# Low parts of three of five up-projection operands: from VectorE to GpSimd, behind the first two differences

## The chip, the cores and the metric

The kernel runs on one core of a Trainium2 chip. The core has five engines with a queue each: TensorE (PE, with its weight loads as PEld), VectorE (DVE), ScalarE (ACT), GpSimd (POOL) and SyncE (SP, which here only starts transfers). Each engine works its queue in order and waits where an operand is not ready. The metric is the device time of one execution in microseconds; several runs are taken and the median is compared.

## The reference

One layer of a hybrid encoder over 1024 positions of width 1024, in float32. After the mixing of tokens comes the part that matters here:

```
h = layer_norm(x) * (1.0 + sc2) + sh2
u = causal_depthwise_conv(h @ w_up, conv_w, conv_b)      # w_up: 1024 x 5632
a, val = split(u, 2)
y = (silu(a) * val) @ w_down                             # 2816 x 1024
x = layer_norm(alpha * x + (1.0 + g2) * y, ln2_g, ln2_b)
```

`h @ w_up` is the up-projection. `h` is its left operand: 1024 positions, in two halves of 512.

## The kernel before

**Two parts of a number.** TensorE multiplies a rounded 32-bit format. To keep the accuracy of float32 the kernel splits each operand in a high part (the operand rounded, made by a cast) and a low part (operand minus high part, a subtraction), and makes three products: high by high, high by low, low by high (`mm3`, `product` at L851, matmuls at L859). A low part is a 128x512 subtraction with both operands in SBUF, the core's on-chip memory.

**Seven products in place of eight.** The up-projection is done by a scheme of Strassen's kind over 2x2 blocks: position halves by halves of the 1024 inputs. From the first half of the positions come `h_11` and `h_21`; from the second half come `h_22` and, by differences with the first, `h_t1 = x - h11`, `h_t2 = y - t1`, `h_t3 = y - x` and `h_t4 = h21 - t2`, where x and y are the two blocks of the second half. Each operand is four 128x512 tiles (`k` or `j` = 0 to 3) with a high and a low part.

**How they are made.** `turned_1` (L1028) is a generator of four steps. Step j loads two tiles of the first half back from memory (SP queue), transposes two blocks on TensorE into PSUM (its accumulator memory), moves them to SBUF with ScalarE (`turned`, L1006: tiles `h`), and calls `put` five times. `put` (L1010) takes a triple of engines: the first makes the difference (L1013, tile `ht`), the second the cast to the high part (L1015, tile `hc`), the third the low part (L1016, tile `hc`). Tiles `h` have four buffers, `ht` six, `hf` (the reloaded ones) four.

**What runs beside them.** The eight `head` calls (L884) do the products of `h_11` and `h_21` with one block of weights each, which need nothing of the second half: two chains of twelve matmuls per head. The weights of a head are loaded by SP, cast by ScalarE (L847) and get their low parts from VectorE (L848, called from `ready`, L868, with `lo=ve`; tiles `wh`, `wl`). A head's results go from PSUM to SBUF by ScalarE (L894) and by a VectorE addition that reads PSUM (L897, tile `mc`). The first step of `turned_1` is issued ahead of the head with number 2, and the three others behind the heads 2, 3 and 4:

```
turns = turned_1(x1)
next(turns)
for c in range(EARLY, HEAD):      # 2 to 7
    head(c)
    next(turns, None)
```

**What follows.** Then come 22 blocks (`Block`, L1159), the rest of the up-projection and the convolution. The first block uses `h_t2`, `h_t1`, `h_t3`, `h_22`, `h_t4` in this order. The weights of the blocks get their low parts from GpSimd (L848 with `lo=po`, tiles `wx`, `wh`, `wl`). Most `wx` tiles lie in memory that the pools of the steps have given back.

**What sets the order.** The program is traced in the order of the code, and a planner then orders the instructions of each engine's queue once, before the run: by the order of the code where an instruction can start by its model of the costs, and with later instructions moved ahead where it can't. Semaphores between the engines are set by the data and by the reuse of buffers. On the chip each queue stays as it was planned.

Of the kernel before, what the change touches and what calls it, by code (L numbers as in the profile page):

```python
# [15 lines left out]
ALU = mybir.AluOpType  # L16
# [28 lines left out]
def body(ctx, tc, a, out):  # L45
    nc = tc.nc
    ve, se, pe, po, sy = nc.vector, nc.scalar, nc.tensor, nc.gpsimd, nc.sync
    uid = [0]

    def nm(s):  # L50
        uid[0] += 1
        return f"{s}_{uid[0]}"

    def opened(**kw):
        cm = tc.tile_pool(reuse_waits="tile", **kw)
        return cm, cm.__enter__()
# [139 lines left out]
    def halves(half):  # L196
        return slice(half * H, (half + 1) * H)
# [615 lines left out]
    def operands(pool, name):  # L813
        return [[pool.tile([P, H], F32R, name=f"{name}{c}{k}", tag=f"{name}{c}{k}") for c in range(2)] for k in range(4)]
# [87 lines left out]
    if True:  # L902
# [98 lines left out]
        def turned(tiles, j, psp=mxt, tag="tt"):  # L1001
            ps = psp.tile([P, H], F32, name=nm("pst"), tag=tag)
            for t in range(4):
                pe.transpose(ps[:, t * P : (t + 1) * P], tiles[t][:, j * P : (j + 1) * P], ident)
            h32 = mxb.tile([P, H], F32, name=nm("h32"), tag="h32", bufs=4)
            se.activation(out=h32, in_=ps, func=AF.Identity, scale=modc[:, 4 * KD + j : 4 * KD + j + 1],  # L1006
                          bias=modc[:, 3 * KD + j : 3 * KD + j + 1])
            return h32

        def put(dst, x, y=None, op=None, e=(ve, ve, po), pool=mxb, n=2):  # L1010
            if y is not None:
                t = pool.tile([P, H], F32, name=nm("ht"), tag="ht", bufs=n)
                e[0].tensor_tensor(out=t, in0=x, in1=y, op=op)  # L1013
                x = t
            (e[1].copy if e[1] is se else e[1].tensor_copy)(out=dst[0], in_=x)  # L1015
            e[2].tensor_sub(out=dst[1], in0=x, in1=dst[0])  # L1016
            return x
# [10 lines left out]
        def turned_1(tiles):  # L1028
            for j in range(4):
                h11, h21 = [th.tile([P, H], F32, name=nm("hf"), tag="hf", bufs=4) for _ in range(2)]  # L1030
                sy.dma_start(out=h11, in_=hx[j])
                sy.dma_start(out=h21, in_=hx[j + 4])
                x, y = turned(tiles, j), turned(tiles, j + 4)
                put(h_22[j], y, e=(None, se, ve))
                t1 = put(h_t1[j], x, h11, ALU.subtract, (ve, se, ve), th, 6)
                t2 = put(h_t2[j], y, t1, ALU.subtract, (ve, se, ve), th, 6)
                put(h_t3[j], y, x, ALU.subtract, (ve, se, ve), th, 6)
                put(h_t4[j], h21, t2, ALU.subtract, (ve, se, ve), th, 6)
                yield

        m0 = merge(0, o0, iter(()))
# [43 lines left out]
    h_22, h_t1, h_t2, h_t3, h_t4 = [operands(hbp, f"hc{i}") for i in range(5)]  # L1085
    th_cm, th = opened(name="th", bufs=2)
    turns = turned_1(x1)
    next(turns)
    start = summed(order[0], slice(0, 4, 3), hbp, "fs"), raw(order[1], 1, hbp, "fs")
# [206 lines left out]
    with tc.tile_pool(name="dn", bufs=2, reuse_waits="tile") as dn:  # L1296
# [44 lines left out]
        for p in products:  # L1341
# [27 lines left out]
            for t in range(4):  # L1369
                for w in ws:  # L1370
                    down(ps, t, w, False, w is ws[-1], not fresh)
                if p == "P4":
                    z = dn.tile([P, H], F32, name=nm("z"), tag="z", bufs=2)
                    y, n0 = ys[4 + t], halves(0)
# [12 lines left out]
            elif p in ("P3", "P2", "P7"):  # L1387
                for t in range(4):
                    x = {"P3": u2, "P2": p1, "P7": p5}[p][t]
# [70 lines left out]
```

## Time and profile before

| what | us |
|---|---|
| runs: median (lowest to highest of 3) | 1549.76 (1547.07 to 1550.41) |
| profiled execution: span from first to last instruction | 1548.2 |
| profiled execution: time beside its span | none given; the span lies within the runs |
| TensorE busy (share of the span) | 1502.7 (97%) |
| VectorE | 1034.5 (67%) |
| ScalarE | 709.5 (46%) |
| GpSimd | 658.2 (43%) |

The profile is of one execution. Instructions are named by engine, line and tiles (`out<-in`), with buffer numbers left out; the many matmuls of L859 are therefore told apart by their weights' tile (`wh`, `wl`, `wx`) and by `ha`, `hb` (the first half's operands) and `hc` (the five of the second half). A time in front of a row is its start from the beginning of the span. In brackets behind a row stands how long the engine sat idle before it, and what it waited for. The mean granted clock of TensorE is 1.00 at full speed.

### The profile page before, as it was taken

How to read it: one execution, taken by the hardware profiler on the slowest of the kernel's cores; microseconds unless marked ns; L12 is line 12 of the kernel's file. 1: busy time of each engine (PE TensorE's matmuls, PEld its weight loads, DVE VectorE, ACT ScalarE, POOL GpSimd, SP SyncE). 2: the span in 40 equal slices, each digit the busy share in tenths (PEclk: the TensorE clock that was granted, in tenths of full speed). 3: DMA queues.
4: the chain of work that ended last, by engine and by line, in shares of the span. 5: the costliest groups of instructions: out<-in, count | busy, mean ns of one | idle time of the engine just before them, and what ended most of it. 6: DMA issues, size and time to landing. Idle time of an engine off the chain costs nothing.

```text
span 1548.2 us, 21760 instructions
## 1 busy us (share of the span) xinstructions
PE 1502.7 (97%) x7663; PEld 1264.7 (82%) x7663; DVE 1034.5 (67%) x2038; ACT 709.5 (46%) x1316; POOL 658.2 (43%) x607
## 2 busy tenths in 40 slices
PE   6999999999999999999998999999999999999996
PEld 3788898889889888888886877888888888888885
DVE  6756566566656565554468587777778776845798
ACT  3545555554544454442112165544544554555451
POOL 0039897787878776730000005454455443000000
PEclk9999999999999999999999999999999999999998
DMA  9156666756576578758999575443344322697552
GB/s 366 50 165 215 217 192 198 218 194 216 189 233 220 189 260 299 260 151 292 308 323 347 214 258 190 140 154 132 122 140 147 115 102 104 246 328 255 191 190 75
DMA packets 129756, 317.54 MB, mean 205 GB/s; under 512 B 13024, under 2 KB 21936, under 8 KB 129648
## 3 DMA queue, kind: packets, MB, share of 16 engines
q1 hardware_dynamic: 90208, 197.83, 37.8%
q0 software_dynamic: 25344, 92.02, 17.8%
q10 hardware_dynamic: 14096, 26.31, 4.8%
q8 instruction: 60, 0.98, 0.3%
q14 instruction: 48, 0.39, 0.1%
HBM read 223.47 MB, written 84.25 MB: 199 GB/s over the span
## 4 chain that ended last, share of the span: by engine, by line
PE 72%; POOL 9%; DMA 8%; DVE 7%; issue 2%; ACT 1%; SPq 0%; ACTq 0%; DVEq 0%; POOLq 0%
PE psu L859 25%; PE psd L1277 4%; PE psd L1278 4%; PE psd L1276 4%; PE pso L508 3%; DMA wod<-dr 3%; PE psg L192 3%; PE psg L194 3%; PE psg L193 3%; POOL dr L553 2%; PE pst L494 2%; POOL acc L559 2%; POOL dr L556 2%; PE psq L194 2%; DMA brd<-dr 2%
## 5 line engine op out<-in xcount | busy, mean ns | idle before, releaser
L859 PE MATMUL psu<-hc,wx 128*128 128x512 f32 x792 | 185.7, 389 | 0.1
L859 PEld LDWEIGHTS psu<-hc,wx 128*128 128x128 f32 x792 | 148.6, 188 | 31.3 <-ACT u L1202 0.5
L1125 DVE SCALAR_TENSOR_TENSOR pcv<-u,convp,pcv 128x1024 f32<-128x1024 f32 x88 | 113.1, 1286 | 45.4 <-ACT pcv L1123 44.4
L1266 DVE TENSOR_TENSOR op<-rw,op 128x512 fp32r<-128x512 f32 x146 | 93.4, 687 | 52.8 <-ACT op L1265 52.5
L1265 ACT CAST op<-rw 128x512 fp32r<-128x512 f32 x146 | 85.2, 622 | 85.4 <-PE psd L1278 39.8
L457 ACT ACTIVATE s<-s,mx 128x640 f32<-128x640 f32 (+7 forms) x128 | 94.5, 738 | 58.6 <-DVE mx L451 57.4
L1277 PE MATMUL psd<-op,op 128*128 128x512 f32 x292 | 113.6, 389 | 0.9 <-DVE op L1266 0.9
L1278 PE MATMUL psd<-op,op 128*128 128x512 f32 x292 | 113.6, 389 | 0.0
L1276 PE MATMUL psd<-op,op 128*128 128x512 f32 x292 | 113.1, 389 | 0.0
L497 ACT CAST pt<-pst 128x512 fp32r<-128x512 f32 (+1 forms) x192 | 82.1, 450 | 62.3 <-PE pst L494 60.8
L498 DVE TENSOR_TENSOR pt<-pst,pt 128x512 fp32r<-128x512 f32 (+1 forms) x192 | 96.0, 519 | 17.2 <-ACT pt L497 15.5
L192 PE MATMUL psq<-h1h,wh 128*128 128x512 f32 x256 | 103.8, 407 | 1.7 <-DVE h1h L188 1.3
L192 PE MATMUL psg<-h1h,wh 128*128 128x512 f32 x256 | 103.7, 405 | 0.0
L194 PE MATMUL psq<-h1h,wl 128*128 128x512 f32 x256 | 100.9, 394 | 0.9 <-DVE wl L112 0.9
L194 PE MATMUL psg<-h1h,wl 128*128 128x512 f32 x256 | 100.3, 392 | 0.5 <-DVE wl L112 0.5
L193 PE MATMUL psq<-h1l,wh 128*128 128x512 f32 x256 | 100.8, 394 | 0.0
L193 PE MATMUL psg<-h1l,wh 128*128 128x512 f32 x256 | 100.2, 391 | 0.0
L556 POOL TENSOR_SCALAR dr<-dr,cond 128x512 f32<-128x512 f32 x56 | 89.9, 1607 | 8.1 <-DMA dr<-in_w_ada 7.1
L508 PE MATMUL pso<-pt,vs 128*128 128x256 f32 x608 | 90.4, 288 | 1.3 <-DVE pt L498 1.2
L994 POOL DMA_DIRECT2D xd<-xr x8 | 4.4, 545 | 199.3 <-DVE xr L992 199.3
L508 PEld LDWEIGHTS pso<-pt,vs 128*128 128x128 f32 x608 | 81.1, 191 | 8.7 <-DVE pt L498 2.6
L112 DVE TENSOR_TENSOR wl<-ws,wh 128x1024 fp32r<-128x1024 f32 x38 | 61.2, 1611 | 39.1 <-ACT wh L111 39.1
(286 smaller groups left out, 4001.3 us busy)
## 6 DMA issues: line engine op xcount, KB each, us to landing
ws<-in_w_up SPq DMA_DIRECT2D x34, 512.0 KB, 3.7
dr<-in_w_ada POOLq DMA_DIRECT2D x32, 512.0 KB, 4.8
dr<-in_w_down POOLq DMA_DIRECT2D x22, 512.0 KB, 4.8
td<-dr POOLq DMA_DIRECT2D x22, 512.0 KB, 4.7
rw<-td SPq DMA_DIRECT2D x44, 256.0 KB, 4.5
yd<-y SPq DMA_DIRECT2D x20, 512.0 KB, 2.7
rw<-yd SPq DMA_DIRECT2D x40, 256.0 KB, 4.2
rw<-sd SPq DMA_DIRECT2D x33, 256.0 KB, 4.6
```

The costliest lines, as they stand in the source:

```text
L192: pe.matmul(ps, wh, xh, start=start, stop=False)
L193: pe.matmul(ps, wh, xl, start=False, stop=False)
L194: pe.matmul(ps, wl, xh, start=False, stop=stop)
L457: se.activation(out=st[:, 0:nk], in_=st[:, 0:nk], func=AF.Exp, scale=-1.0, bias=prev, accum_out=sums[:, col : col + 1])
L498: ve.tensor_sub(out=dl, in0=src, in1=dh)
L508: pe.matmul(ps[:, 0:256], vs[:, h % 2, j0 + j, :], pt[j // 4][:, c, j % 4, :], start=j == 0 and c == 0, stop=j == nj - 1 and c == 1)
L556: po.tensor_scalar_mul(x[:, k % 2, :] if k else acc, x[:, k % 2, :], cond[:, k : k + 1])
L859: pe.matmul(ps, w[:, a_, k, :], h[k][b_], start=first, stop=k == 3 and a_ == 1, skip_group_check=on)
L1125: ve.scalar_tensor_tensor(out=ps, in0=u[b][:, 2 - d : S + 2 - d], scalar=cp[:, 2 - d : 3 - d], in1=ps, op0=ALU.mult, op1=ALU.add)
L1276: pe.matmul(ps[t], g[:, 0, ts], d[:, 0], start=start, stop=False, skip_group_check=on)
L1277: pe.matmul(ps[t], g[:, 0, ts], d[:, 1], start=False, stop=False, skip_group_check=on)
L1278: pe.matmul(ps[t], g[:, 1, ts], d[:, 0], start=False, stop=stop, skip_group_check=on)
```

## The change

In each of the four steps the `put` of `h_22` moves from in front of `h_t1` and `h_t2` to behind them, and the low parts of `h_22`, `h_t3` and `h_t4` are subtracted by GpSimd (`po`) where VectorE (`ve`) did it. The differences stay on VectorE, the casts on ScalarE. In all twelve 128x512 subtractions change their engine, four casts and their subtractions change their place. No transfer, no buffer and no arithmetic changes.

```
                 x, y = turned(tiles, j), turned(tiles, j + 4)
-                put(h_22[j], y, e=(None, se, ve))
                 t1 = put(h_t1[j], x, h11, ALU.subtract, (ve, se, ve), th, 6)
                 t2 = put(h_t2[j], y, t1, ALU.subtract, (ve, se, ve), th, 6)
-                put(h_t3[j], y, x, ALU.subtract, (ve, se, ve), th, 6)
-                put(h_t4[j], h21, t2, ALU.subtract, (ve, se, ve), th, 6)
+                put(h_22[j], y, e=(None, se, po))
+                put(h_t3[j], y, x, ALU.subtract, (ve, se, po), th, 6)
+                put(h_t4[j], h21, t2, ALU.subtract, (ve, se, po), th, 6)
                 yield
```

## The prediction

> **What bounds the kernel now.** I read the page first (span and busy shares), then the busy time by stretches of time, to find the stage that the change touches, then the chain of work that ended last in that stage, and last the order of single instructions there.
>
> ```profile
> span 1548.2 us, 21760 instructions
> PE 1502.7 (97%) x7663; PEld 1264.7 (82%) x7663; DVE 1034.5 (67%) x2038; ACT 709.5 (46%) x1316; POOL 658.2 (43%) x607
> ```
>
> TensorE is busy for 97% of the span, so a change that only moves VectorE work pays only where TensorE waits for VectorE. The low parts of the five operands are made between 918 and 946 us (columns: length, then busy time and count of PE, PEld, DVE, ACT, POOL, then the granted clock, DMA share, GB/s):
>
> ```profile
> 905.00:918.00 13.00, 13.00 (x62) 10.41 (x61) 9.90 (x41) 8.41 (x14) 0.53 (x1) 1.00 0.91 308
> 918.00:946.00 28.00, 24.55 (x110) 19.16 (x109) 27.18 (x45) 23.37 (x43) 0.98 (x1) 0.94 0.56 192
> 946.00:978.00 32.00, 31.95 (x142) 26.09 (x141) 17.38 (x19) 15.09 (x23) 22.87 (x21) 1.00 0.49 167
> 1020.00:1320.00 300.00, 300.00 (x1325) 248.50 (x1324) 224.99 (x236) 148.70 (x212) 142.15 (x105) 1.00 0.37 128
> ```
>
> In this stretch, and not before or behind it, VectorE is the full engine: 27.18 of 28 us. TensorE has 3.45 us of idle time (28 - 24.55) and GpSimd does nothing until its end. Behind it TensorE runs without a gap (31.95 of 32, 300 of 300), so whatever is won or lost at 946 us reaches the end. The chain agrees: it leaves TensorE here, goes from difference (L1013) to low part (L1016) to the heads' weights (L848) on VectorE, and returns to TensorE at 945.02:
>
> ```profile
> 922.61 0.69 DVE hc L1016
> ...
> 944.37 0.61 DVE wh L848
> 944.98 0.04 issue
> 945.02 31.55 PE psu L859 x138
> ```
>
> TensorE's own row order shows what it waits for:
>
> ```profile
> 928.90 0.66 PE L1004 MATMUL pst<-ident,x 128*128 128x128 f32 x4 [1.10 <-ACT h L1006]
> 931.18 4.15 PE L859 MATMUL psu<-ha,wh 128*128 128x512 f32 x10 [1.63 <-DVE wh L848]
> 935.17 2.47 PE L859 MATMUL psu<-hb,wl 128*128 128x512 f32 x10
> 938.77 2.81 PE L859 MATMUL psu<-ha,wh 128*128 128x512 f32 x11 [0.22 <-ACT wh L847]
> 945.02 2.60 PE L859 MATMUL psu<-ha,wh 128*128 128x512 f32 x10 [0.50 <-DVE wh L848]
> ```
>
> It waits for low parts of the **heads'** weights, which stand in VectorE's queue behind the operands' differences. The ten products at 931.18 took 4.15 us where ten take 2.47 at 935.17: 1.7 us lost to a lower granted clock (0.55, next row).
>
> ```profile
> 931.20:935.00 3.80, 3.80 (x10) 2.97 (x11) 3.80 (x7) 3.02 (x6) 0.00 (x0) 0.55 0.74 259
> ```
>
> So the most that any relief of VectorE can win here is 3.45 + 1.7 = 5.15 us (0.33%).
>
> **What the change takes off VectorE.** These groups stand between 917 and 947 us:
>
> ```profile
> L1016 DVE TENSOR_TENSOR hc<-ht,hc 128x512 fp32r<-128x512 f32 x16 | 10.7, 685 | 0.3 <-ACT hc L1015 0.3
> L1016 DVE TENSOR_TENSOR hc<-h,hc 128x512 fp32r<-128x512 f32 x4 | 2.7, 685 | 0.0
> L897 DVE TENSOR_TENSOR mc<-psu,mc 128x512 f32<-128x512 f32 x4 | 2.7, 684 | 0.0
> ```
>
> Of the 20 low parts (four steps of five) 12 move: the four from h (h_22) and eight of the sixteen from ht (h_t3, h_t4). Between them stand 16 differences, 7 low parts of weights and 4 additions from PSUM: 20 + 16 + 7 + 4 = 47. An instruction lasts 0.68 us, but the next starts 0.60 later:
>
> ```profile
> 934.05 0.68 DVE L1013 TENSOR_TENSOR ht<-h,ht 128x512 f32<-128x512 f32 x1
> 934.65 0.68 DVE L1016 TENSOR_TENSOR hc<-ht,hc 128x512 fp32r<-128x512 f32 x1
> 935.25 0.68 DVE L1013 TENSOR_TENSOR ht<-h,h 128x512 f32<-128x512 f32 x1
> ```
>
> 47 x 0.60 = 28.2 us, and with some 0.9 us of waits that is the way from 918.05 to 947.29. Taking 12 away saves 12 x 0.60 = **7.2 us**, if nothing else happened.
>
> **What it puts in their place.** GpSimd subtractions of this form last 1.28 us undisturbed, and GpSimd has room for 12 of them (15.4 of 28 us). The question is what they do to VectorE. A little later both engines work at once, and these rows show it:
>
> ```profile
> 955.04 1.28 POOL L848 TENSOR_TENSOR wl<-ws,wl 128x512 fp32r<-128x512 f32 x1
> 956.29 1.74 POOL L848 TENSOR_TENSOR wl<-s,wl 128x512 fp32r<-128x512 f32 x1
> 957.99 1.75 POOL L848 TENSOR_TENSOR wx<-wt,wx 128x512 fp32r<-128x512 f32 x1
> ```
>
> ```profile
> 955.11 1.76 DVE L845 TENSOR_TENSOR wt<-ws,s 128x512 f32<-128x512 f32 x1 [1.77 <-POOL wh L848]
> 956.80 1.78 DVE L845 TENSOR_TENSOR wt<-ws,ws 128x512 f32<-128x512 f32 x1
> 958.50 0.68 DVE L1157 TENSOR_TENSOR u<-psu,p 128x512 f32<-128x512 f32 x1
> ```
>
> A VectorE instruction with two operands in SBUF that starts behind a GpSimd subtraction takes 1.76 and 1.78 us in place of 0.68, GpSimd's next takes 1.74 in place of 1.28, and the two alternate. From 955.11 to 956.80 VectorE needs 1.69 us for what takes it 0.60 alone: **1.09 us** for each GpSimd subtraction that it meets. The addition from PSUM at 958.50 runs at 0.68 beside the GpSimd subtraction of 957.99 and pays nothing. In the changed stretch 31 of VectorE's 35 instructions have both operands in SBUF.
>
> The Trainium skill, page "SBUF — State Buffer", section "Who interferes with whom", has a rule against this change: a VectorE instruction with two SBUF inputs contends with a GpSimd instruction that reads SBUF, and the second to issue blocks until the first is done. Taken literally, with the whole 1.28 us of the row lost for each, it would give 12 x 1.28 - 7.2 = 8.2 us slower; the rows show the same lock at 1.09. The rows decide.
>
> The other bound is a case in which VectorE loses nothing:
>
> ```profile
> 944.88 1.29 DVE L1016 TENSOR_TENSOR hc<-ht,hc 128x512 fp32r<-128x512 f32 x2
> 946.09 0.69 DVE L848 TENSOR_TENSOR wl<-ws,wl 128x512 fp32r<-128x512 f32 x1
> 946.69 0.68 DVE L897 TENSOR_TENSOR mc<-psu,mc 128x512 f32<-128x512 f32 x1
> ```
>
> ```profile
> 945.02 2.91 POOL L848 TENSOR_TENSOR wh<-ws,wh 128x512 fp32r<-128x512 f32 x1 [35.85 <-DMA p<-md]
> ```
>
> Here GpSimd, idle for long, started at 945.02, and three VectorE subtractions went on at their 0.60 while it took 2.91 us. The price of one is therefore between 0 and 1.09 us. I take the upper, because it is the steady case: this is GpSimd's first work in the stage, and where it was already running a pair of VectorE instructions back to back did yield:
>
> ```profile
> 1045.88 0.68 DVE L1145 TENSOR_TENSOR sc<-y 128x512 f32<-128x512 f32 x1
> 1046.48 1.77 DVE L845 TENSOR_TENSOR wt<-ws,ws 128x512 f32<-128x512 f32 x1
> ```
>
> ```profile
> 1046.25 1.46 POOL L848 TENSOR_TENSOR wl<-s,wl 128x512 fp32r<-128x512 f32 x1 [1.44 <-ACT wl L847]
> ```
>
> **The rest of the change.** h_22's cast on ScalarE (0.62 us, four of them) and its subtraction move behind the casts of t1 and t2 of their step. ScalarE waits for VectorE's differences anyway in this stretch:
>
> ```profile
> ACT hc L1015 <- DVE ht L1013: 4.3, 6, 1.6
> ```
>
> I cost that move at nothing; if its cover were gone, it would be at most 4 x 0.62 = 2.5 us on ScalarE. No DMA moves. What is queued behind the moved work: on GpSimd, the low part of 945.02 and the first three `wx` of the blocks, which TensorE needs from 949.73 on (three took 4.12 us, so the first is done only about then); on VectorE, the heads' weights, for which TensorE waits at 931.18 and 945.02. GpSimd also returns the h and ht buffers later, but with four and six of them a step has about one step (7 us) to return them.
>
> ```profile
> 948.02 4.12 POOL L848 TENSOR_TENSOR wx<-ws,wx 128x512 fp32r<-128x512 f32 x3
> ```
>
> ```profile
> 949.73 5.60 PE L859 MATMUL psu<-hc,wx 128*128 128x512 f32 x24
> ```
>
> **The sum.** VectorE's stretch: -12 x 0.60 + 12 x 1.09 = -7.2 + 13.1 = +5.9 us. The four additions from PSUM can run under a GpSimd subtraction, 0 to 4 x 0.60 = 2.4 us; I take half, -1.2. Together **+4.7 us**. TensorE follows, since it waits for weights on that queue, and GpSimd's last subtraction pushes the blocks' `wx` the same way. The profiled span of 1548.2 becomes 1552.9; the page gives no other time for that execution, and the median of the runs is 1.56 us above it: 1549.76 + 4.7 = **1554.5 us**.
>
> **Rivals.**
>
> *VectorE keeps its turn* (as at 945.02). GpSimd then finds its place in the gaps, VectorE's stretch shrinks by 7.2 us, TensorE is the bound, and of the 5.15 us I would expect all but the last half microsecond of waiting: 1549.76 - 4.6 = 1545.2. For it: three undisturbed subtractions. Against it: the alternation at 955 and 1046. It decides from a mean price below 0.60 us per GpSimd subtraction, where the exchange stops costing. 0.10.
>
> *The heads' weights get ahead.* The instruction order is a planner's. If it now puts the heads' low parts some two places earlier in VectorE's queue, TensorE's waits at 931 and 945 do not grow, and only the blocks' start feels the late differences and the late `wx`: two places of 1.69 us back from 4.7 leaves 4.7 - 3.4 = +1.3, 1551.1. For it: with three instructions fewer per step VectorE runs out of ready work sooner. Against it: in the present order a head's weights stand behind the differences of a step, near its end. 0.24.
>
> *Everything late falls together.* No PSUM addition covers anything (+5.9), GpSimd's first subtraction takes the 2.91 us of 945.02 and VectorE pays the excess (2.91 - 1.28 = 1.6), and longer waits of TensorE bring the 1.7 us of the lower clock in front of the last head, where nothing hides them (today a wait for the next weights at 938.77 follows it): 5.9 + 1.6 + 1.7 = +9.2, 1559.0. 0.08.
>
> **How the numbers follow.** The forecast has 0.58. About 0.2% (3.1 us) is what a measurement can tell from no change here, so the limits are 1546.7 and 1552.9: faster 0.10 (first rival), same 0.24 (second), slower 0.66 (forecast and third). Range: from the second rival downwards by as much as it varies with one more place (1.7 us; 1549.4) and a little of the way to the first, 1548.5, up to the third's 1559.0; it leaves out the first rival and some of the tails. The forecast's own range is 1552.5 to 1557.5.
>
> **What would show it.** Right: 12 GpSimd subtractions at L1016 of 1.3 to 1.8 us; VectorE's L1013 and remaining L1016 and L848 in the stretch with a mean well over 0.68, many near 1.7; TensorE waiting longer for the heads' weights, and the blocks' first products (949.73 today) at about 954 to 955. Wrong: VectorE still at 0.68 there and the blocks starting near 945 (first rival); slow VectorE instructions but no longer wait of TensorE (second). If the stretch is longer by another cause, a wait for buffers or for ScalarE's casts, the step that put the price on the shared operands was wrong.

## The result and the profile after

| | before | after |
|---|---|---|
| median of 6 runs (lowest to highest), us | 1548.41 (1545.48 to 1550.41) | 1555.44 (1552.20 to 1558.62) |
| ratio, with its 95% interval | | 1.0047 [1.0032, 1.0062] |
| span of the profiled execution, us | 1548.2 | 1550.0 |

The changed kernel is 0.47% slower, some 7 us. Predicted were 1554.5 us, 4.7 us more than the 1549.76 that the forecast set out from. The two profiled spans differ by only 1.8 us, and the reason matters for the reading: in this execution the changed kernel reached the first product of the heads at 890.17 us and the kernel before at 895.55. Those 5.4 us were won in work that the diff does not touch. So the stage is compared by its own length, from the first product of the heads to the first product of the blocks. First the busy shares of the changed kernel, from its page:

```profile
PE 1503.7 (97%) x7663; PEld 1265.4 (82%) x7663; DVE 1038.5 (67%) x2026; ACT 709.0 (46%) x1316; POOL 674.2 (43%) x619
```

VectorE has twelve instructions less (2026 against 2038) and is busy for 4 us longer. Then busy time by stretches: the stage in the kernel before, and in the changed one, followed there by the stretch behind it (columns as in the prediction):

```profile
895.55:949.73 54.18, 50.55 (x227) 39.92 (x226) 49.01 (x107) 38.98 (x67) 5.41 (x9) 0.97 0.69 233
```

```profile
890.17:951.64 61.47, 53.06 (x227) 40.78 (x226) 52.90 (x95) 37.77 (x64) 23.85 (x21) 0.92 0.65 212
...
978.00:1018.00 40.00, 40.00 (x178) 33.16 (x177) 33.25 (x36) 19.06 (x28) 21.67 (x18) 1.00 0.42 139
```

The stage takes 61.47 us in place of 54.18: **+7.3 us**, which is what the timed ratio says. Of this, TensorE's idle time is (61.47 - 53.06) - (54.18 - 50.55) = 8.41 - 3.63 = 4.8 us, and the same 227 matmuls take 53.06 - 50.55 = 2.5 us longer at a lower clock (0.92 against 0.97). Behind it TensorE is full as before (40.00 of 40.00 us), and next to nothing is given back: 0.4 us on the way to the down-projection (table below).

What GpSimd and VectorE do to each other, in groups of instructions by shape (count, busy us, mean ns):

```profile
L1016 POOL TENSOR_TENSOR hc<-ht,hc 128x512 fp32r<-128x512 f32 x8 | 13.0, 1641 | 4.4 <-ACT hc L1015 4.4
L1016 POOL TENSOR_TENSOR hc<-h,hc 128x512 fp32r<-128x512 f32 x4 | 6.4, 1598 | 17.8 <-ACT hc L1015 14.5 <-issue 3.3
...
L848 DVE TENSOR_TENSOR wh<-ws,wh 128x512 fp32r<-128x512 f32 x5 | 6.1, 1228 | 1.1 <-ACT wh L847 1.1
L1013 DVE TENSOR_TENSOR ht<-hf,ht 128x512 f32<-128x512 f32 x4 | 4.9, 1234 | 0.0
L897 DVE TENSOR_TENSOR mc<-psu,mc 128x512 f32<-128x512 f32 x7 | 4.8, 683 | 0.2 <-ACT mc L894 0.2
```

Twelve GpSimd subtractions last 1.6 us in the mean. VectorE's subtractions with two operands in SBUF go from 0.685 to as much as 1.23 us; the additions from PSUM (L897) stay at 0.683. Single instructions of the two engines, in order of time:

```profile
919.21 1.74 POOL L1016 TENSOR_TENSOR hc<-h,hc 128x512 fp32r<-128x512 f32 x1
920.92 1.71 POOL L1016 TENSOR_TENSOR hc<-ht,hc 128x512 fp32r<-128x512 f32 x1
```

```profile
918.02 1.79 DVE L1016 TENSOR_TENSOR hc<-ht,hc 128x512 fp32r<-128x512 f32 x1
919.73 1.77 DVE L1013 TENSOR_TENSOR ht<-h,hf 128x512 f32<-128x512 f32 x1
921.43 0.68 DVE L897 TENSOR_TENSOR mc<-psu,mc 128x512 f32<-128x512 f32 x1
...
925.52 1.76 DVE L848 TENSOR_TENSOR wh<-ws,wh 128x512 fp32r<-128x512 f32 x1
...
944.02 1.72 DVE L848 TENSOR_TENSOR wh<-ws,wh 128x512 fp32r<-128x512 f32 x1
```

This is the alternation that the prediction read at 955 us, now in the middle of the stage, and it falls on the heads' weights too (925.52, 944.02). From VectorE's first difference to the end of the last head's `wh` it takes 33.04 us (912.70 to 945.74) where it took 26.92 (918.05 to 944.97). In that part of the queue stand 34 instructions in place of 43, worth 9 x 0.60 = 5.4 us less; eleven of them are stretched, by 10.2 us together; and VectorE has 1.0 us more of idle time. That makes 10.2 - 5.4 + 1.0 = 5.8 of the 6.1 us. TensorE's row order shows where it arrives:

```profile
925.61 1.22 PE L859 MATMUL psu<-hb,wl 128*128 128x512 f32 x2 [4.06 <-ACT wl L847]
...
935.58 0.74 PE L859 MATMUL psu<-ha,wh 128*128 128x512 f32 x2 [0.88 <-ACT wh L847]
...
944.04 0.88 PE L859 MATMUL psu<-ha,wh 128*128 128x512 f32 x2 [2.06 <-ACT wh L847]
...
945.79 3.52 PE L859 MATMUL psu<-ha,wh 128*128 128x512 f32 x10 [0.43 <-DVE wh L848]
...
951.64 1.52 PE L859 MATMUL psu<-hc,wx 128*128 128x512 f32 x6
```

Before, TensorE waited for weights mainly where VectorE's low parts were late (1.63 and 0.50 us). Now its long waits are for **ScalarE's casts** of the heads' weights (4.06, 0.88, 2.06), and the ten products in front of the blocks take 3.52 us where they took 2.60. What ScalarE itself waits for, in one of its rows:

```profile
933.95 0.62 ACT L1015 CAST hc<-ht 128x512 fp32r<-128x512 f32 x1 [1.85 <-DVE ht L1013]
```

and the sum of it, from the waits of all engines between 909 and 953 us (us in total, times, longest):

```profile
ACT hc L1015 <- DVE ht L1013: 9.3, 9, 1.9
...
PE psu L859 <- ACT wl L847: 4.1, 1, 4.1
...
PE psu L859 <- ACT wh L847: 2.9, 2, 2.1
...
PE psu L859 <- DVE wh L848: 1.2, 3, 0.5
```

The cast of a head's weights stands in ScalarE's queue behind the cast of a step's last difference, and that difference is one of the instructions that VectorE gets through late (L1013 `ht<-hf,ht`, mean 1234 ns). Between the two, ScalarE starts the store of a head's result (L898), for which it waits until VectorE's addition (L897) is done. ScalarE's waits for differences grew from 4.3 to 9.3 us, and TensorE's long waits came to be for ScalarE. The bound itself stays on VectorE: from 914.58 to 945.75 us the chain of work that ended last leaves it only once, for the 1.0 us between 934.54 and 935.56:

```profile
932.21 1.71 DVE ht L1013
933.91 0.61 DVE mc L897
934.54 0.33 ACTq L898
...
934.91 0.63 ACT wh L847
...
935.56 1.21 DVE wh L848
```

### The profile page after: what moved, and what is told of

Its sections match the earlier page's. It is cut to its first block, busy times and chain, and to the rows that moved or that the text cites. A ratio compares the mean times of both kernels' runs of the same rounds, so it can differ in the third digit from the quotient of the medians.

```text
span 1550.0 us, 21786 instructions
## 1 busy us (share of the span) xinstructions
PE 1503.7 (97%) x7663; PEld 1265.4 (82%) x7663; DVE 1038.5 (67%) x2026; ACT 709.0 (46%) x1316; POOL 674.2 (43%) x619
## 4 chain that ended last, share of the span: by engine, by line
PE 87%; DVE 7%; DMA 3%; ACT 1%; issue 1%; SPq 0%; DVEq 0%; ACTq 0%
PE psu L859 26%; PE pso L508 5%; PE psd L1277 4%; PE psd L1278 4%; PE psd L1276 4%; PE psg L192 4%; PE psg L193 4%; PE psg L194 4%; PE pst L494 4%; PE psq L193 3%; PE psq L192 3%; PE psq L194 3%; PE pss L443 2%; PE pss L442 2%; PE psv L295 2%; PE psv L294 2%
```

## The experiments

Stage is again the way from the first product of the heads to the first product of the blocks in the profiled execution; "behind" is the way from there to the first product of the down-projection (375.73 us before). "Stretched" is the time beyond 0.685 us of VectorE's instructions from the first difference to the last head's `wh`, with their number in brackets. GpSimd subtractions that began later than that `wh` can add nothing to it: one of the twelve in added_reads, one of the eight in only_t3_t4.

| kernel | GpSimd subtractions | stretched, us | stage, us | behind, us | timed ratio to before |
|---|---|---|---|---|---|
| before | 0 | 0 | 54.18 | 375.73 | 1 |
| the change | 12 | 10.23 (11) | 61.47 | 375.36 | 1.0047 [1.0032, 1.0062] |
| added_reads | 12 added | 8.90 (11) | 64.45 | 375.36 | 1.006 [1.0041, 1.008] |
| added_writes | 0 (48 fills) | 0 | 54.90 | 375.36 | 0.9988 [0.9973, 1.0003] |
| order_only | 0 | 0.58 (1) | 57.27 | 376.32 | 1.000 [0.9981, 1.0019] |
| no_reads | 0 (12 fills) | 0 | 51.70 | 379.69 | 0.9991 [0.9973, 1.0008] |
| engine_only | 12 | 11.33 (11) | 64.54 | 375.41 | 1.0055 [1.004, 1.007] |
| only_t3_t4 | 8 | 6.43 (7) | 57.20 | 377.87 | 1.0019 [1.0006, 1.0031] |
| only_h22 | 4 | 3.23 (4) | 55.85 | 377.19 | 1.0012 [0.9996, 1.0029] |
| steps_later | 0 | 0 | 52.76 | 380.18 | 1.0022 [1.001, 1.0035] |
| later_slots | 0 | 0 | 49.10 | 377.88 | 0.9987 [0.9967, 1.0006] |
| slots_only | 0 | 0 | 53.98 | 376.02 | 0.9984 [0.9965, 1.0003] |

The theory under test: each GpSimd subtraction that meets VectorE's two-operand work costs VectorE more than the 0.60 us that it saves. The main rivals: GpSimd's activity as such, the moved place of h_22, or the order that the planner made of it.

**Reads or activity: added_reads and added_writes.** Both leave the queues of TensorE, VectorE and ScalarE as in the kernel before (a spare tile takes the results).

```
-                put(h_t4[j], h21, t2, ALU.subtract, (ve, se, ve), th, 6)
+                put(h_t4[j], ...); [po.tensor_sub(out=spare, in0=src, in1=src)
+                    for src in (h_t1[j][0], h_t2[j][0], h_t3[j][0])]     # added_reads
+                put(h_t4[j], ...); [po.memset(spare.bitcast(F32), 0.0)
+                    for _ in range(12)]                                   # added_writes
```

> The kernel before, with twelve GpSimd subtractions added (three behind each step's differences) that read high parts of h_t1, h_t2, h_t3 and write a spare tile nobody reads. The queues of all other engines hold the same instructions in the same order as before. Theory A (a GpSimd subtraction and a VectorE instruction with two SBUF operands exclude each other): VectorE loses 1.09 us for each of the twelve, 13.1 us, less up to 4 x 0.60 = 2.4 us under the additions from PSUM, and less what falls behind the last head's weights (two or three of them, 3 us): the stretch grows by 7 to 11 us, the kernel is 0.45 to 0.7% slower, VectorE's subtractions there show durations near 1.7 us. Theory B (the loss of the changed kernel comes from its new plan, above all from casts of heads' weights that stand behind the differences in ScalarE's queue): the plan here is the old one, so no change, within 0.2%.

> The kernel before, with 48 GpSimd memsets of a spare 128x512 tile added at the same place, which write SBUF and read nothing; the other queues are the same as before. Theory A (it is the read side that is shared): VectorE's subtractions stay at 0.68 us and the time within 0.2% of before. Rival (any work of GpSimd slows VectorE): some 48 x 0.5 us of GpSimd work stretch VectorE's by several us, 0.3% or more. Theory B: no change.

Twelve added GpSimd subtractions alone, with nothing taken off VectorE, cost 0.6%, and eleven VectorE instructions are stretched by 8.9 us, 0.74 for each subtraction. TensorE here waits 6.5 us for VectorE's low parts and 2.3 us for ScalarE's casts: the way by ScalarE belongs to the changed kernel's order, and the loss comes without it too. Rows of added_reads, first GpSimd's earliest subtraction and two later ones in a row, then a VectorE instruction that began under those two:

```profile
920.68 1.04 POOL L1038 TENSOR_TENSOR spare<-hc 128x512 fp32r<-128x512 f32 x1 [11.84 <-ACT hc L1015]
...
938.72 2.75 POOL L1038 TENSOR_TENSOR spare<-hc 128x512 fp32r<-128x512 f32 x2 [4.35 <-ACT hc L1015]
```

```profile
939.05 1.52 DVE L1016 TENSOR_TENSOR hc<-ht,hc 128x512 fp32r<-128x512 f32 x1
```

In added_writes GpSimd filled a tile 48 times, one after the other, and VectorE's subtractions under it kept 0.69 us. First GpSimd's row, then VectorE's:

```profile
906.70 28.02 POOL L1038 MEMSET spare<- 128x512 f32 x48
```

```profile
924.98 0.69 DVE L1016 TENSOR_TENSOR hc<-ht,hc 128x512 fp32r<-128x512 f32 x1
```

So it is not that GpSimd works, nor that it writes; what the subtractions have and the fills lack is reads. The fills ran ahead of their steps, from 906.7 to 934.7 us, so VectorE's rows behind 934.7 us were not under them; the rows before that show no trace of it.

**Place or engine: order_only, engine_only and no_reads.** order_only moves h_22 and leaves all low parts on VectorE; engine_only leaves h_22 in front and moves the twelve low parts to GpSimd; no_reads is the changed kernel with the twelve subtractions on GpSimd replaced by fills.

```
-                put(h_22[j], y, e=(None, se, po))                # order_only: after with
+                put(h_22[j], y, e=(None, se, ve))                # ve for all three

-                put(h_22[j], y, e=(None, se, ve))                # engine_only: before with
+                put(h_22[j], y, e=(None, se, po))                # po for h_22, h_t3, h_t4

-            e[2].tensor_sub(out=dst[1], in0=x, in1=dst[0])       # no_reads, on after
+            e[2].tensor_sub(...) if e[2] is ve else po.memset(dst[1].bitcast(F32), 0.0)
```

> The changed kernel with all five low parts left on VectorE: only the place of h_22 behind the first two differences is changed. Theory A: no GpSimd reads, VectorE has its 47 instructions as before: within 0.2% of before (plus or minus 2 us by the new plan). Theory B (new plan): a good part of the 7 us loss of the changed kernel, 3 us or more.

> The change without its move: h_22 stays in front of the first two differences, the twelve low parts go to GpSimd. TensorE's queue is that of the changed kernel. Theory A (each GpSimd subtraction costs VectorE about 0.9 us and saves it 0.60): the loss of the changed kernel again, TensorE's way from the first head's product to the first block's product 5 to 9 us longer than before, 0.3 to 0.6% slower. If the move behind the differences made the loss: within 0.2% of before.

> The changed kernel with its twelve GpSimd subtractions replaced by twelve memsets of the low parts (this leaves the low parts of h_22, h_t3 and h_t4 out of the result, they are zero). The queues have the order of the changed kernel but for neighbouring pairs behind the stretch. Theory A: VectorE is relieved of twelve subtractions and nobody contends: TensorE becomes the bound, the kernel is 3 to 5 us faster than before (0.2 to 0.33%), and 10 us or more faster than the changed one. Theory B (plan): the waits of TensorE for ScalarE's casts stay, and the kernel is still slower than before by 3 us or more.

The place alone has no measurable effect, 1.000 [0.9981, 1.0019]. (Its one profile shows a stage 3.1 us longer, with a window of low clock just in front of the blocks; the timed runs do not repeat it in their median.) The engine alone costs 0.55%, about as much as the whole change, so the place of h_22 is not the cause. It is not a burden either: with h_22 in front TensorE waits for the last head's cast for 4.27 us, against 2.06 in the changed kernel:

```profile
950.96 1.22 PE L859 MATMUL psu<-ha,wh 128*128 128x512 f32 x2 [4.27 <-ACT wh L847]
```

no_reads has TensorE's order of the changed kernel and the other queues all but so. Its stage is 51.70 us against 61.47: the twelve subtractions cost 9.8 us of the stage, with the waits and the lower clock that they bring. (The fills wait for nothing and ran from 908.8 to 914.5 us, ahead of VectorE's differences, so this run takes away the overlap together with the reads; added_reads and added_writes keep the two apart.) That the same order without the reads loses nothing also speaks against the planner's order as the cause. And no_reads shows what the relief is worth when nothing is paid for it: 54.18 - 51.70 = 2.5 us at the start of the blocks. But the time did not fall (0.9991 [0.9973, 1.0008]), because the first block then waits. TensorE's rows of no_reads, and behind them the part of the chain of waits that led there:

```profile
946.91 5.60 PE L859 MATMUL psu<-hc,wx 128*128 128x512 f32 x24
954.98 4.58 PE L859 MATMUL psu<-hc,wh 128*128 128x512 f32 x12 [2.46 <-ACT wx L847]
```

```profile
941.93 0.61 DVE wl L848
...
942.56 5.37 DMA ws<-in_w_up
...
952.49 1.75 DVE wt L845
...
954.26 0.63 ACT wx L847
```

The next load of weights from memory starts when the last head's `wl` gives its buffer free (942.56), takes 5.37 us and is followed by a sum, a cast and the product. TensorE is 2.5 us early there, waits 2.46 us and runs twelve products in 4.58 us at the lower clock. All of the relief is gone again.

**How the price grows: only_t3_t4 and only_h22.** The changed kernel with one of its two kinds of low parts back on VectorE.

```
-                put(h_22[j], y, e=(None, se, po))                          # only_t3_t4
+                put(h_22[j], y, e=(None, se, ve))

-                put(h_t3[j], y, x, ALU.subtract, (ve, se, po), th, 6)      # only_h22: ve for
-                put(h_t4[j], h21, t2, ALU.subtract, (ve, se, po), th, 6)   # both of these
```

> The changed kernel with the low part of h_22 back on VectorE: eight GpSimd subtractions in place of twelve. Theory A: eight at about 0.93 - 0.60 = 0.33 us net, 2.6 us, and two thirds of the 2.5 us of waits that came with them: TensorE's way to the first block 3 to 6 us longer than before, 0.2 to 0.4% slower. Rival (one late GpSimd result or one unlucky place in the plan makes all of the loss): either nothing or all 7 us.

> The changed kernel with the low parts of h_t3 and h_t4 back on VectorE: h_22 stands behind t1 and t2 as in the change, and only its four low parts are GpSimd's. Theory (each GpSimd subtraction that meets VectorE's two-operand instructions costs VectorE 0.8 to 0.95 us and gives it 0.60 back): an excess of 3 to 4 us on 3 or 4 VectorE instructions, VectorE's stretch 0.8 to 1.4 us longer than with all low parts on VectorE, ratio to the kernel before 1.000 to 1.002. Rival (what costs is not the single subtraction but GpSimd's standing at work for long, several in a row): four single ones cost nothing, excess under 1 us, ratio 0.998 to 1.000. Rival (the cost has a fixed part, such as the lower clock, that comes with the first few): ratio 1.003 or more.

Four, eight and twelve subtractions stretch VectorE by 3.23, 6.43 and 10.23 us: 0.81, 0.80 and 0.85 us each (of the eight, the seven that count cost 0.92). The price is one per subtraction, not a fixed one, and in all three it lies above the 0.60 us that each takes off. The times follow in order (1.0012, 1.0019, 1.0047), though four of them can't be told from none: the interval of only_h22 holds 1. (In only_h22 and only_t3_t4 the way behind the stage is 1.5 and 2.1 us longer as well; why was not followed up.) That its price per subtraction is the same speaks against the rival that only rows of several in a row cost.

**Relief without GpSimd: steps_later, later_slots, slots_only.** If VectorE's queue in front of the heads' weights is the bound, issuing the steps one head later should win up to the 5.15 us that the prediction gave as the limit.

```
     for c in range(EARLY, HEAD):
         head(c)
-        next(turns, None)
+        next(turns, None) if c > EARLY else None      # steps_later and later_slots
+    [next(slots) for _ in range(6)]                    # later_slots and slots_only
```

> The kernel before, all low parts on VectorE, with the second, third and fourth step issued behind heads 3, 4 and 5 in place of 2, 3 and 4. The heads' weights then stand in VectorE's queue ahead of a step's differences. If VectorE's order is what makes TensorE wait in this stretch, the waits of 3.45 us there shrink to 1 us or less: 2 to 4 us less to the first block's product. How much of it reaches the end depends on the next load of weights, which starts only when the last head's buffer is free: with the give-back that the kernel without reads showed (2.5 us of wait behind the first block's products) nothing would be left, without it the kernel is 0.15 to 0.25% faster than before.

> The kernel before, with steps 2 to 4 of the operands issued one head later (behind heads 3, 4 and 5), and the round of tiles for the blocks' weights turned on by six places, so that the first block's weights go to the tiles wh and wl of the heads and not to the tiles wx that lie in the steps' old memory. The later steps alone gave 1.0022: heads without waits, but 3.32 and 2.28 us of waiting in the first block for wx. Theory (what was won at the heads is given back because the wx tiles lie in memory that the steps free late): the first block starts without these two waits, stage from first head product to first block product some 49 to 51 us, ratio 0.996 to 0.999. Rival (the first block waits for its weights whatever tile they go to, since their load and casts stand behind the last steps in the queues): 2 us or more of waiting stay in the first block, ratio 1.001 to 1.003.

> The kernel before with nothing but the round of tiles for the blocks' weights turned on by six places. Theory (the first block's weights are not what the kernel before waits for, the heads' low parts on VectorE are): ratio 0.999 to 1.001, stage 53.5 to 55 us. Rival (the tiles wx are late in the kernel before too): ratio 0.997 or less.

steps_later clears the heads and is slower, 1.0022 [1.001, 1.0035]. TensorE's rows of steps_later:

```profile
943.11 2.43 PE L859 MATMUL psu<-hb,wl 128*128 128x512 f32 x10
948.86 0.73 PE L859 MATMUL psu<-hc,wx 128*128 128x512 f32 x2 [3.32 <-ACT wx L847]
951.87 6.50 PE L859 MATMUL psu<-hc,wx 128*128 128x512 f32 x18 [2.28 <-POOL wx L848]
```

The heads end at 945.5 us, and the first block waits 5.6 us for its weights, whose `wx` tiles lie in the memory that the steps give back. later_slots puts the first block's weights in the heads' own tiles `wh` and `wl` instead:

```profile
939.63 2.43 PE L859 MATMUL psu<-hb,wl 128*128 128x512 f32 x10
941.90 2.43 PE L859 MATMUL psu<-hc,wh 128*128 128x512 f32 x10
944.85 0.73 PE L859 MATMUL psu<-hc,wh 128*128 128x512 f32 x2 [0.53 <-DVE hc L1016]
...
949.30 0.96 PE L859 MATMUL psu<-ha,wx 128*128 128x512 f32 x3 [0.52 <-POOL wx L848]
```

Now the blocks follow the heads without a gap, the stage is 49.10 us, 5.1 less than before, and 2.2 us of it are given back behind (two waits of 0.5 us stand in these rows; the first is for an operand, not for weights). slots_only shows that the turn of the tiles alone leaves the stage as it was (53.98). later_slots is the quickest by its profile (span 1542.0 us), but its ratio of 0.9987 [0.9967, 1.0006] can't be told from no change, so none of these kernels is shown to beat the kernel before; against the kernel before, it stands clear of the changed kernel's 1.0047.

## Why the prediction was right

*The bound.* Right: TensorE waits in this stage for the heads' weights, and what is lost there reaches the end (stage +7.3 us, behind it -0.4). The limit of 5.15 us for any relief was reached and not passed: later_slots wins 5.1 us in the stage.

*What the change takes off VectorE, 12 x 0.60 = 7.2 us.* Too large in its place: 5.4. TensorE's waits end with the last head's `wh`, and two of the sixteen low parts from ht already stood behind that (at 944.88 in the kernel before), while one other addition (L1195) now stands ahead of it. Ten less and one more make nine.

*The price, 1.09 us for each, less 1.2 for the additions from PSUM: 11.9 us.* Right in kind and close in size: 10.2 us on eleven instructions, 0.85 for each of the twelve. The alternation at 1.7 us was there (918.02, 919.73), the additions from PSUM at 0.68 under a GpSimd subtraction as well (921.43). Eight of the twelve cost VectorE 1.04 to 1.12 us each, the forecast price. Of the other four, which met an addition from PSUM or VectorE's own wait, three cost 0.47 to 0.60 and one nothing. The Trainium skill's rule ("SBUF — State Buffer", section "Who interferes with whom") is borne out in who meets whom: reads against two-operand work (added_reads), not fills (added_writes). Its literal price of one whole GpSimd subtraction, 1.28 us, is above all that was measured here, 1.12 at the most.

*The other bound, that VectorE keeps its turn.* In the changed kernel it did not occur: the first subtraction, after 10.6 us of idle time, took 1.29 us, not the 2.91 seen at 945.02, and the VectorE instruction that began beside it took 1.80. But it is real. In only_t3_t4 the first subtraction took 5.18 us, while six of VectorE's subtractions in a row kept their 0.60. It ended 1.22 us behind the start of the addition from PSUM (930.62), and the next VectorE instruction was stretched:

```profile
926.66 5.18 POOL L1016 TENSOR_TENSOR hc<-ht,hc 128x512 fp32r<-128x512 f32 x1 [14.56 <-PE psu L859]
```

```profile
930.62 0.68 DVE L897 TENSOR_TENSOR mc<-psu,mc 128x512 f32<-128x512 f32 x1
931.23 1.16 DVE L848 TENSOR_TENSOR wh<-ws,wh 128x512 fp32r<-128x512 f32 x1
```

Nor was the case at 945.02, which the prediction read as one in which VectorE loses nothing, quite free: the VectorE instruction behind its addition from PSUM, at 947.29 (L1195), took 1.18 us, and 0.68 in no_reads, where no GpSimd subtraction ran beside it. What decides which engine gets the turn is not shown.

*The sum of the two.* -5.4 + 10.2 = +4.8 against the forecast's +4.7. Both terms were too large, by 1.8 and 1.7 us, and the errors cancelled: that is luck. So is a part of the nearness of 1554.5 to the measured 1555.44 us: the kernel before came out at 1548.41 in place of the 1549.76 that the sum set out from, so the slowdown was forecast at 4.7 us and measured at some 7.

*The step that fell short: "ScalarE waits for VectorE's differences anyway".* The move of h_22, costed at nothing, did cost nothing by itself (order_only 1.000). And TensorE did follow VectorE's queue: the last wait in front of the blocks is again for VectorE's `wh` (0.43 us at 945.79). But ScalarE was looked at only for its four moved casts, and its waits for VectorE's differences (4.3 us) were taken as cover. They are a path: behind a late difference stands the cast of a head's weights, and TensorE came to wait 7.0 us for these casts (4.1 + 2.9), where it had waited for weights mainly by VectorE's low parts. Most of that lay beside VectorE's own lateness. What it added to the way to the blocks is the 1.1 us for which VectorE in its turn waited for one of ScalarE's `wh` (in the group of L848 `wh` above), 1.0 us more idle time in all.

*The lower clock.* The forecast left it out and put it (1.7 us) into the rival in which everything late falls together. It happened: the last head's ten products took 3.52 us, and over the stage the lower clock cost 2.5 us more than before. A part of it lay under VectorE's lateness and delayed nothing; what counts is the way behind the last head's `wh`, from 945.79 to 951.64, 5.85 us where it was 4.71 (945.02 to 949.73). Of these 1.1 us, 0.9 are the slower ten products and 0.2 one product more behind the wait. With them, the 1.0 us of VectorE's wait and 0.3 us that no group accounts for, 4.8 becomes 7.2.

*The rivals.* VectorE keeps its turn: refuted for the changed kernel by the rows. The heads' weights get ahead: refuted; they stand behind the differences as before and are stretched themselves (925.52, 927 and 944.02), and on ScalarE they fell further back. Everything late together (+9.2) was near in size but had one of its three parts, the lower clock, and that at 0.9 us in place of 1.7: the additions from PSUM did cover, and the first subtraction took 1.29 us.

*What would show it.* The twelve GpSimd subtractions of 1.27 to 1.74 us and VectorE's rows near 1.7 are there. The wait for ScalarE's casts was named among the signs that the price on the shared operands was wrong; it came in addition to that price and as its consequence. The blocks' first products were forecast at 954 to 955 us and stand at 951.64; measured from the heads' first product, as it must be with a lead of 5.4 us, they stand at 957.0 of the earlier clock.

## What to carry to other kernels

Handing one of two engines' equal subtractions to an idle engine helps only if the two do not hold each other up: here each 0.60 us taken off VectorE put 0.80 to 0.94 us back on it, which rows of a later stage had shown before the change. Look for the exchange rate in the trace, then follow the late instruction through every queue it feeds, the casts of a third engine among them. And a relief of the bound is worth what the next stage can take up: three kernels here started the blocks 1.4 to 5.1 us earlier and lost 2.2 to 4.5 us behind that, two of them to weights whose memory came free too late.

## What the runs showed of the hardware

*The clock.* In these profiles the lower clock (0.50) comes in windows of 3.41 us on a fixed grid, and a window behind one at full clock is low when TensorE was busy for less than about 45% of that one. Busy time by stretches of the changed kernel, cut at these windows (the first number behind the length is TensorE's busy time, the third from the end its clock):

```profile
920.57:923.98 3.41, 0.98 (x5) 0.48 (x3) 3.41 (x5) 1.24 (x2) 2.06 (x2) 1.00 0.62 169
923.98:927.39 3.41, 1.28 (x3) 0.56 (x3) 3.41 (x5) 2.90 (x5) 2.27 (x2) 0.50 0.65 212
927.39:930.81 3.42, 3.42 (x11) 2.75 (x12) 3.29 (x4) 1.67 (x4) 1.03 (x1) 0.50 0.35 92
941.05:944.46 3.41, 1.35 (x7) 0.74 (x5) 3.41 (x4) 1.70 (x4) 3.41 (x3) 1.00 0.86 328
944.46:947.88 3.42, 2.99 (x8) 1.99 (x7) 3.42 (x3) 1.05 (x3) 2.22 (x6) 0.50 0.22 84
```

29% busy, then low; the low window itself was 38% busy, and the next was low once more; 40%, then low. In engine_only a window with 1.83 us of 3.42 (54%) was followed by full clock:

```profile
939.20:942.62 3.42, 1.83 (x8) 1.37 (x8) 2.37 (x4) 2.42 (x5) 1.12 (x1) 1.00 0.20 77
942.62:946.03 3.41, 3.41 (x16) 2.81 (x15) 3.28 (x5) 2.69 (x7) 2.27 (x2) 1.00 0.70 255
```

Counted over the twelve profiles, without their first 100 and last 15 us, 29 of 29 windows at full clock with under 44% were followed by a low one, 16 of 16 with 49 to 62% by a full one, and of three between them two by a low one. Behind a low window the mark lies higher: 12 of 12 low windows that were 33 to 82% busy were followed by another low one, 31 of 31 from 86% on by a full one. The Trainium skill, "TensorE: Matmul & The Clock Gate", section "What's actually happening", gives the window's length (3.4 us) and that it runs free, with which these rows agree; it speaks of an idle window, and in the changed kernel the windows ahead of the low ones were 29 to 40% busy. A wait of 2 us can so cost another 1.7 us, or nothing, by where it falls on the grid. That this explains part of the spread among runs of one kernel is likely but was not tried.

*The price by length.* GpSimd's subtraction with one tile as both inputs lasted 1.04 us where it was the first to start (920.68 in added_reads; 1.28 with two tiles), and a VectorE instruction that waits behind it is 1.52 us long, not 1.76. The price went with the length of the GpSimd instruction.
